# The tenth weight chunk of a feed-forward's down product as seven block products

## The chip, the cores and the metric

One core of one Trainium2 chip. The metric is the device time of one execution in microseconds (us), as the median of several runs; lower is better. The core's engines work side by side, each through its own list of instructions in program order: TensorE (PE: matmuls and the weight loads PEld), VectorE (DVE), ScalarE (ACT), GpSimd (POOL), and SyncE (SP), which issues most DMA transfers.

## The reference, cut to what matters

A decoder layer on 256 tokens of width 1024: pooling and attention heads, cross-attention, then a gated feed-forward of inner width 2816, each followed by a residual and a layer norm. The change touches the last product only:

```python
def swiglu(h, w_gate, w_up, w_down):
    return (jax.nn.silu(h @ w_gate) * (h @ w_up)) @ w_down

h = layer_norm(DEEPNORM_ALPHA * h + swiglu(h, w_gate[l], w_up[l], w_down[l]), ln3_g[l], ln3_b[l])
```

All tensors are float32. The kernel keeps that accuracy by splitting each operand into a high part (a cast to a shorter format, by ScalarE) and a low part (the operand minus its high part, by VectorE); one product then is three matmuls: high by high, high by low, low by high.

## The kernel before

**Tiles of the last product.** The inner width 2816 is cut into 11 chunks c = 0 to 10 of 256, each two row groups of 128 of `w_down`. The output is four pieces, C11 and C12 (tokens 0 to 127, left and right 512 columns), C21 and C22 (tokens 128 to 255). For a chunk the gated activations are four 128x128 blocks A11, A12, A21, A22 (token half, row group), the weights four 128x512 blocks B11, B12, B21, B22 (row group, column half). Done plainly, a chunk is eight block products, two for each piece.

**Seven products.** Chunks 0 to 8 (`SEVEN = 9`) use a scheme with seven. Three go to shared sums and are `shared_products(c)` together with A11·B11: four products from two prepared tiles x and y (left half of x is B11, its right half a sum of blocks; y holds two sums). `four(c, c+1)` makes the two products of the plain lower row (A12·B21 into C11, a token sum S4 by B22 into C12), `fourth` the one of A22 with a fourth weight sum into C21. The token sums S1 to S4 are formed by GpSimd (`token_sums`, lines 1098 to 1103) and split by ScalarE and VectorE (`token_sums_split`, `fourth_split`). The weight sums are formed in place by `Stream.sums` (lines 84 to 101): two casts of 512 columns and one of 1024 on ScalarE, six VectorE operations of 512 columns and one of 1024. `merge()` adds the shared sums up into `merged[0..3]` for the four pieces. Chunks 9 and 10 are plain: their four row groups run as `rest` through each piece at the end of `down()`, C22 in two column pieces of 256.

**Order of the weight work.** `Stream` holds one list of items in the order in which their tiles are prepared: `whole` (a row group: load, cast, low part), `sums` and `made` (the two tiles of a pair of rows), `home` (the tile of a fourth sum, kept meanwhile in a free buffer: those of chunks 0 to 7 in the norm's buffers `r`, `g`, `b`, that of chunk 8 in a raw buffer). Each product calls `ws.get`, and this calls `tick`, which prepares the next item only while fewer than `AHEAD = 9` tiles lie ahead of those used up; a `sums` needs room for two. Raw rows have 7 buffers, and `fetch` issues a load on SyncE's queue as soon as one counts as free. A tile wN is item N, and its parts are wNh (high), wNl (low), wNr (raw). Here w115 to w118 are the last weights of gate and up, w119 and w120 the sums of chunk 8, w121 onwards is down.

**Gate and up, then down.** A loop over c makes the gated chunk c on TensorE (48 matmuls of 512 columns), and behind it `shared_products(c - 2)`. Its last turn is c = 10. Then `down()` is stepped with `run(dn, 1)`, one product a step, and a table `events` puts splits, the return of the last gated chunk (`gated_in`) and parts of `merge` ahead of given steps. Behind the seven-product chunks, two VectorE additions (lines 1273 and 1274) put `merged` into the banks of C12 and C21 in place; then the rest is run piece by piece: C11, C12, the fourth products of chunks 4 to 7 (`LATE = 4`), C21, C22 in two halves. Each piece's layer norm follows on VectorE while TensorE runs the next.

**Buffers that matter.** `sg` (gated), `sraw` (raw token sums), `S` (split sums) and `u` (merged) share one ring of 6 buffers of tag `pr`, in the order in which they are made.

Of the kernel before, what the change touches and what calls it, by code (L numbers as in the profile page):

```python
# [17 lines left out]
T = S // P  # L18
# [6 lines left out]
NFC = DFF // CW  # L25
# [9 lines left out]
BUSY = 7  # L35
SEVEN, LAG, LATE = 9, 2, 4
GROUPED = 3
# [6 lines left out]
class Stream:  # L44


    def __init__(self, nc, pool):
        self.nc, self.pool = nc, pool
        self.src, self.raws, self.tiles, self.homes = [], [], [], []
        self.loads, self.splits = {}, {}  # L50
        self.used, self.held = 0, True
        self.pace, self.asked = 1, 0
        self.cuts, self.steps = {}, {}
        self.items, self.freed, self.rest = [], 0, {}
        self.kept = set()

# [73 lines left out]
    def prepare(self, upto, now=False):  # L130
        nc = self.nc
        while len(self.tiles) < min(upto, len(self.items)):
# [6 lines left out]
            if kind == "whole":  # L139
                self.fetch(r + 1, nc.sync)  # L140
                raw = self.raws[r]
                hi = self.pool.tile(list(raw.shape), F32R, tag="hi", name=f"w{i}h")
                lo = self.pool.tile(list(raw.shape), F32R, tag="lo", name=f"w{i}l")
                whole = [slice(0, raw.shape[2])]
                casts, subs = self.steps.get(r, (whole, whole))
                for s in casts:
                    nc.scalar.copy(hi[:, :, s], raw[:, :, s])
                for s in subs:
                    nc.vector.tensor_sub(lo[:, :, s], raw[:, :, s], r32(hi[:, :, s]))
                self.tiles.append((hi, lo))  # L150
                self.freed = r + 1
            elif kind == "sums":
                self.fetch(r + 2, nc.sync)
                self.tiles += self.sums(i, r)
                self.freed = r + (1 if r in self.kept else 2)
            else:
                raw, (hi, lo) = r(), self.part(i)
                self.freed += len(self.kept)
                self.kept.clear()
# [50 lines left out]
def decoder_layer(  # L210
# [68 lines left out]

    c_gu, c_sums = [], []  # L280
    for c in range(NFC):
        c_gu.append(ws.add(w_gu[c], 4))
        n = c - LAG
        if 0 <= n < SEVEN:
            c_sums.append(ws.add_sums([row(2 * n), row(2 * n + 1)], (lambda n=n: t4_home(n)) if n < SEVEN - 1 else None))
    c_t4, c_low = {}, {}
    c_t4[SEVEN - 1] = ws.add_home(lambda: ws.rest[ws.items[c_sums[-1][0][0]][1]]())
    c_low[SEVEN - 1] = ws.add(row(2 * SEVEN - 1), 1)
    for n in range(0, SEVEN - 1, 2):
        home = lambda n=n: t4[n // 2]  # L290
        if n < LATE:
            c_t4[n] = ws.add_home(home)
        for c in (n, n + 1):
            c_low[c] = ws.add(row(2 * c + 1), 1)
        if n >= LATE:
            c_t4[n] = ws.add_home(home)
    c_dn = {c: [ws.add(row(2 * c + f), 1) for f in range(2)] for c in range(SEVEN, NFC)}


# [791 lines left out]
    def token_sums(c):  # L1091
# [9 lines left out]
        own = s_raw[c][:, :, 3, :]  # L1101
        s4_raw = own if c == SEVEN - 1 else s_raw["fourth"][:, c].rearrange("p (i b) -> p i b", i=4)
        nc.gpsimd.tensor_sub(s4_raw, a12, s2)  # L1103

    def token_sums_split(c):
        hl = [sp.tile([P, 4, P], F32R, name=f"S{n}", tag="pr", bufs=PR_BUFS) for n in range(2)]
        sums_of[c] = [(hl[0][:, m], hl[1][:, m]) for m in range(3)]
        n = 3
        if c == SEVEN - 1:
            s4[c], n = (hl[0][:, 3], hl[1][:, 3]), 4  # L1110
# [66 lines left out]
    for c in range(1, NFC):  # L1177
# [6 lines left out]
        if c > 1:  # L1184
            gated_split(c - 2)
            if c - 2 < SEVEN:
                token_sums(c - 2)
        run(gu, 2)
        gated_in(c - 1)
        run(gu, 1)  # L1190
        if 0 <= c - 2 < SEVEN:
            token_sums_split(c - 2)
# [7 lines left out]
        if c == NFC - 1:  # L1200
            gated_out(c)
            residual(1)
        if 0 <= c - LAG < SEVEN:
            shared_products(c - LAG)
# [30 lines left out]
    def merge():  # L1235

        p1, p5, p6, p7 = shared
        for t in range(T):
            norms.append(Norm(3, h2[:, t, :]))

# [16 lines left out]
    def down():  # L1257

        yield from fourth(SEVEN - 1, SEVEN)
        yield from four(SEVEN - 1, SEVEN)  # L1260
        for c in range(0, SEVEN - 1, 2):
            if c < LATE:
                yield from fourth(c, c + 2)
            yield from four(c, c + 2)
        load_norm("g", 3, ln3_g)()
        load_norm("b", 3, ln3_b)()
# [8 lines left out]
        for piece in (*PIECES[:3], (1, 512, LAST), (1, LAST, D)):  # L1275
            t, c0, c1 = piece
            if piece == PIECES[2]:
                for c in range(LATE, SEVEN - 1, 2):
                    yield from fourth(c, c + 2)
# [136 lines left out]
```

## Time and profile before

| | us |
|---|---|
| median of 3 runs | 364.32 (364.13 to 364.88) |
| the profiled execution | 364.02 |
| its span, first to last instruction | 362.2 |
| TensorE busy | 356.8 (98%) |
| VectorE busy | 313.1 (86%) |
| ScalarE busy | 201.9 (56%) |
| GpSimd busy | 61.0 (17%) |

All times in the rows are of the one profiled execution, counted from the start of its span. Matmuls are pipelined, so that a row of 0.39 us is the time of one from issue to its modelled end; the distance from one start to the next is what it takes of TensorE's time. A mean busy share is taken over stages with different limits; the timelines of the engines show single instructions, and in brackets how long the engine stood idle before one and what ended that.

### The profile page before, as it was taken

Reading aid. Unit: us, or ns where it says so; the run is one execution under the profiler, and the core shown is the slowest. Engines: PE = TensorE matmul, PEld = TensorE weight load, DVE = VectorE, ACT = ScalarE, POOL = GpSimd, SP = SyncE. Lnnn points to the kernel's source line nnn. Section 1 sums busy time; section 2 is a strip of 40 time slices with the busy share of each in tenths; the row PEclk is TensorE's granted clock in tenths of the full one; section 3 lists DMA queues with packets and bytes.
Section 4 is the critical chain, followed back from the end, with each engine's and each line's share of the span. In section 5 each row is a group of like instructions: output and inputs, shape, how many; then the busy total and the mean of one; then the engine's idle time right before and its main releaser. Section 6 shows DMA issues by size and latency. Waiting matters only on the chain.

```text
span 362.2 us, 5435 instructions
## 1 busy us (share of the span) xinstructions
PE 356.8 (98%) x1843; PEld 304.4 (84%) x1843; DVE 313.1 (86%) x477; ACT 201.9 (56%) x317; POOL 61.0 (17%) x82
## 2 busy tenths in 40 slices
PE   8999999999999999999999999999999999999995
PEld 7887888888888899988888888888888888888884
DVE  5878999985999888775879989999998999879984
ACT  5857776375362765465037636744754754679301
POOL 1000009400000003320110024225303413400000
PEclk9999999999999999999999999999999999999999
DMA  7997388799936996943107887888879779658211
GB/s 247 419 419 281 116 286 314 227 329 316 371 148 208 375 373 219 340 137 135 58 0 239 320 283 243 292 293 302 297 253 346 246 256 313 218 172 260 85 58 58
DMA packets 35771, 89.22 MB, mean 246 GB/s; under 512 B 4256, under 2 KB 14368, under 8 KB 35616
## 3 DMA queue, kind: packets, MB, share of 16 engines
q1 hardware_dynamic: 34544, 86.92, 68.5%
q0 software_dynamic: 624, 1.57, 1.3%
q10 hardware_dynamic: 576, 0.39, 0.3%
q8 instruction: 14, 0.23, 0.2%
q14 instruction: 13, 0.11, 0.1%
HBM read 81.53 MB, written 7.34 MB: 245 GB/s over the span
## 4 chain that ended last, share of the span: by engine, by line
PE 98%; DMA 1%; ACT 0%; ACTq 0%; issue 0%
PE pg L376 11%; PE pg L375 11%; PE pg L374 11%; PE pxq L392 6%; PE pqk L548 6%; PE acc L374 6%; PE acc L376 6%; PE acc L375 6%; PE pxk L418 4%; PE x L376 2%; PE x L375 2%; PE x L374 2%; PE pxk L414 2%; PE pu L418 2%; PE xv L376 2%; PE xv L375 2%
## 5 line engine op out<-in xcount | busy, mean ns | idle before, releaser
L1098 POOL TENSOR_TENSOR sraw<-gr 128x128 f32<-128x128 f32 x9 | 8.7, 962 | 94.8 <-DMA gr<-gd 69.7
L847 POOL TENSOR_TENSOR rs<-mv,mhalf 128x1 f32<-128x1 f32 x6 | 4.4, 731 | 104.3 <-DVE mv L845 104.3
L703 POOL TENSOR_TENSOR win<-upad 128x271 f32<-128x271 f32 x4 | 3.5, 882 | 52.5 <-DVE upad L737 52.5
L478 ACT CAST h2Th<-tp 128x512 fp32r<-128x512 f32 x4 | 2.4, 588 | 14.5 <-PE tp L489 14.5
L1099 POOL TENSOR_TENSOR sraw<-sraw,gr 128x128 f32<-128x128 f32 x9 | 10.2, 1134 | 0.7
L1078 ACT ACTIVATE sg<-pg 128x256 f32<-128x256 f32 x22 | 7.8, 379 | 2.8 <-PE pg L376 2.7
L479 DVE TENSOR_TENSOR gTl<-gr,gTh 128x512 fp32r<-128x512 f32 x11 | 8.6, 780 | 0.7 <-ACT gTh L478 0.7
L478 ACT CAST gTh<-gr 128x512 fp32r<-128x512 f32 x11 | 6.8, 614 | 3.7 <-DMA gr<-gd 3.7
L1100 POOL TENSOR_TENSOR sraw<-gr 128x128 f32<-128x128 f32 x9 | 8.5, 945 | 0.0
L1079 DVE TENSOR_TENSOR sg<-sg,pg 128x256 f32<-128x256 f32 x22 | 8.3, 413 | 0.1
L510 POOL DMA_DIRECT2D xr<-xd x12 | 6.6, 554 | 8.7 <-DMA xd<-xs 6.3
L607 ACT ACTIVATE pr<-pr,mx 128x256 f32<-128x256 f32 (+1 forms) x12 | 5.5, 460 | 4.5 <-DVE mx L653 4.5
L607 ACT ACTIVATE xpr<-xs,mx 128x256 f32<-128x256 f32 x8 | 3.7, 470 | 7.6 <-DVE mx L618 7.6
L499 DVE STREAM_TRANSPOSE gs<-sg 128x512 f32<-128x512 f32 x11 | 7.7, 701 | 0.1
L478 ACT CAST S<-sraw 128x384 fp32r<-128x384 f32 (+1 forms) x9 | 4.7, 523 | 5.0 <-POOL sraw L1100 5.0
L502 POOL DMA_DIRECT2D xd<-xs x3 | 1.9, 629 | 33.4 <-DVE xs L499 33.4
L1336 ACT ACTIVATE minus<-ident 128x128 f32<-128x128 f32 x1 | 0.3, 311 | 12.8 <-DVE r L858 12.8
L852 DVE SCALAR_TENSOR_TENSOR r<-r,mv,g 128x512 f32<-128x512 f32 (+1 forms) x10 | 7.0, 727 | 0.2
L838 DVE BATCH_NORM_STATS2 st<-r 128x6 f32<-128x512 f32 (+1 forms) x10 | 6.4, 637 | 0.3
L1103 POOL TENSOR_TENSOR S<-gr,sraw 128x128 f32<-128x128 f32 x8 | 6.6, 828 | 0.0
L748 ACT COPY pr<-pxk 128x256 f32<-128x256 f32 x8 | 2.6, 376 | 7.2 <-PE pxk L414 7.2
L981 PE MATMUL xs<-xkTh,xq 128*128 128x256 f32 x32 | 6.4, 283 | 0.0
(1363 smaller groups left out, 1409.2 us busy)
## 6 DMA issues: line engine op xcount, KB each, us to landing
gd<-gs SPq DMA_DIRECT2D x11, 256.0 KB, 5.6
gr<-gd SPq DMA_DIRECT2D x44, 64.0 KB, 2.0
pd<-ps SPq DMA_DIRECT2D x4, 384.0 KB, 4.1
pt<-pd SPq DMA_DIRECT2D x16, 96.0 KB, 5.7
g<-in_ln_g SPq DMA_DIRECT2D x3, 512.0 KB, 5.4
b<-in_ln_b SPq DMA_DIRECT2D x3, 512.0 KB, 7.2
wr<-in_w_qkv SPq DMA_DIRECT2D x5, 256.0 KB, 4.6
mr<-in_mem_t SPq DMA_DIRECT2D x1, 1024.0 KB, 11.8
```

The lines of the kernel that those rows point to most:

```text
L374: nc.tensor.matmul(ps, wa, ya, start=start, stop=False, skip_group_check=part)
L375: nc.tensor.matmul(ps, wa, yb, start=False, stop=False, skip_group_check=part)
L376: nc.tensor.matmul(ps, wb, ya, start=False, stop=stop, skip_group_check=part)
L392: nc.tensor.matmul(pss[f], w[:, s], y, start=k == 0 and f == 0 and n == 0, stop=k == KD - 1 and n == 2, skip_group_check=True)
L418: nc.tensor.matmul(pss[f], hi[:, s], both, start=k == 0, stop=False, skip_group_check=True)
L478: nc.scalar.copy(h, ps)
L479: nc.vector.tensor_sub(l, ps, r32(h))
L548: nc.tensor.matmul(qk[i][f][:, n], w[:, c * P:(c + 1) * P], both[:, n], start=k == 0 and n.start == 0 and (n.stop == 2 or part in first), ...
L607: nc.scalar.activation(dst[:, j, :], src[:, j, :], AF.Exp, bias=mx[:, j:j + 1], scale=sign, accum_out=sm[:, j:j + 1])
L1098: nc.gpsimd.tensor_add(s1, a21, a22)
L1099: nc.gpsimd.tensor_sub(s2, s1, a11)
L1100: nc.gpsimd.tensor_sub(s3, a11, a21)
```

## The change

Chunk 9 goes through seven products as well (`SEVEN = 10`), with chunk 10 alone left plain. Its weight sums stand in the middle of down's list, behind the lower rows of chunks 0 to 3, and its fourth sum stays in a raw buffer, as that of chunk 8 does. Its token sums are issued right behind the last gated chunk, its four shared products behind those of chunk 3. The homes of chunks 0 to 3 move from the start of down to its end, and all fourth products of chunks 0 to 7 now run together ahead of C21. The `events` get new steps, and the norm objects are made later. A choice of GpSimd for low parts is added, whose set stays empty.

```diff
-SEVEN, LAG, LATE = 9, 2, 4
+SEVEN, LAG, PAIRED, ASIDE = 10, 2, 8, 9
...
-                    nc.vector.tensor_sub(lo[:, :, s], raw[:, :, s], r32(hi[:, :, s]))
+                    (nc.gpsimd if i in self.helped else nc.vector).tensor_sub(lo[:, :, s], raw[:, :, s], r32(hi[:, :, s]))
...
     c_gu, c_sums = [], []
+
+    def add_sums(n):
+        c_sums.append(ws.add_sums([row(2 * n), row(2 * n + 1)], (lambda: t4_home(n)) if n < PAIRED else None))
+
     for c in range(NFC):
         c_gu.append(ws.add(w_gu[c], 4))
-        n = c - LAG
-        if 0 <= n < SEVEN:
-            c_sums.append(ws.add_sums([row(2 * n), row(2 * n + 1)], (lambda n=n: t4_home(n)) if n < SEVEN - 1 else None))
+        if c >= LAG:
+            add_sums(c - LAG)
     c_t4, c_low = {}, {}
...
-    for n in range(0, SEVEN - 1, 2):
-        home = lambda n=n: t4[n // 2]
-        if n < LATE:
-            c_t4[n] = ws.add_home(home)
-        for c in (n, n + 1):
-            c_low[c] = ws.add(row(2 * c + 1), 1)
-        if n >= LATE:
-            c_t4[n] = ws.add_home(home)
...
+    add_fourth(PAIRED)
+    add_low(PAIRED)
+    for n in range(PAIRED):
+        add_low(n)
+        if n == 3:
+            add_sums(ASIDE)
+            add_fourth(ASIDE)
+            add_low(ASIDE)
+    add_fourth(4)
+    add_fourth(6)
     c_dn = {c: [ws.add(row(2 * c + f), 1) for f in range(2)] for c in range(SEVEN, NFC)}
+    add_fourth(0)
+    add_fourth(2)
...
         if c == NFC - 1:
             gated_out(c)
             residual(1)
-        if 0 <= c - LAG < SEVEN:
+            token_sums(ASIDE)
+        if c >= LAG:
             shared_products(c - LAG)
...
-        yield from fourth(SEVEN - 1, SEVEN)
-        yield from four(SEVEN - 1, SEVEN)
-        for c in range(0, SEVEN - 1, 2):
-            if c < LATE:
-                yield from fourth(c, c + 2)
+        yield from fourth(PAIRED, PAIRED + 1)
+        yield from four(PAIRED, PAIRED + 1)
+        for c in range(0, PAIRED, 2):
             yield from four(c, c + 2)
+            if c == 2:
+                shared_products(ASIDE)
+                yield from fourth(ASIDE, ASIDE + 1)
+                yield from four(ASIDE, ASIDE + 1)
...
             if piece == PIECES[2]:
-                for c in range(LATE, SEVEN - 1, 2):
+                for c in (4, 6, 0, 2):
                     yield from fourth(c, c + 2)
...
     events = {
-        4: lambda: fourth_split(4, SEVEN - 1), 5: lambda: gated_in(NFC - 1), 6: lambda: gated_split(NFC - 2),
-        12: lambda: gated_split(NFC - 1),
+        3: lambda: gated_split(ASIDE), 5: lambda: gated_in(NFC - 1), 7: lambda: token_sums_split(ASIDE),
+        11: lambda: fourth_split(4, PAIRED), 13: lambda: gated_split(NFC - 1),
     }
-    events.update({step: lambda: run(parts, 1) for step in (8, 16, 17)})
-    for step in range(23):
+    events.update({step: lambda: run(parts, 1) for step in (15, 18, 19)})
+    for step in range(22):
...
     until(dn)
+    norms += [Norm(3, h2[:, t, :]) for t in range(T)]
```

## Rows read from the trace of the kernel before

**Rows 1.** The page's engine line and the shares of its chain that ended last.

```profile
PE 356.8 (98%) x1843; PEld 304.4 (84%) x1843; DVE 313.1 (86%) x477; ACT 201.9 (56%) x317; POOL 61.0 (17%) x82
PE 98%; DMA 1%; ACT 0%; ACTq 0%; issue 0%
```

**Rows 2.** One stretch of down: busy us by engine, granted clock, DMA share, GB/s.

```profile
335.00:340.00 5.00, 5.00 (x23) 4.13 (x22) 5.00 (x6) 3.47 (x4) 0.00 (x0) 1.00 0.45 159
```

**Rows 3.** VectorE's timeline in down: start us, us, line, tiles, wait before it.

```profile
324.31 0.71 DVE L499 STREAM_TRANSPOSE gs<-sg 128x512 f32<-128x512 f32 x1
325.36 1.23 DVE L149 TENSOR_TENSOR w127l<-w124r,w127h 128x1024 fp32r<-128x1024 f32 x1 [0.33 <-ACT w127h L147]
342.59 1.28 DVE L1274 TENSOR_TENSOR acc<-u,acc 128x512 f32<-128x512 f32 x2
344.52 0.42 DVE L1303 TENSOR_TENSOR r<-u,acc 128x256 f32<-128x256 f32 x1 [0.65 <-PE acc L1286]
```

**Rows 4.** TensorE's timeline: down, C11, C12, C22, the first matmul behind them, the last.

```profile
325.96 0.39 PE L374 MATMUL acc<-w121h,gTh 128*128 128x512 f32 x1
341.60 0.39 PE L1284 MATMUL acc<-w135h,gTh 128*128 128x512 f32 x1
344.32 0.39 PE L1284 MATMUL acc<-w135h,gTh 128*128 128x512 f32 x1
352.48 0.28 PE L1284 MATMUL acc<-w135h,gTh 128*128 128x256 f32 x1
355.35 1.02 PE L1350 MATMUL left<-r,ident 128*128 128x256 f32 x4
357.80 0.59 PE L1358 MATMUL out<-r,diag 128*128 128x256 f32 x2
```

**Rows 5.** VectorE's timeline: first operation of chunk 8's sums, first operation behind them.

```profile
305.10 0.69 DVE L92 TENSOR_TENSOR w119l<-w119r,w119h 128x512 fp32r<-128x512 f32 x1
310.35 0.74 DVE L1079 TENSOR_TENSOR sg<-sg,pg 128x256 f32<-128x256 f32 x2
```

**Rows 6.** VectorE's timeline: splits of 512 and of 1024 columns with GpSimd idle.

```profile
332.78 0.68 DVE L479 TENSOR_TENSOR gTl<-gr,gTh 128x512 fp32r<-128x512 f32 x1
333.38 1.22 DVE L149 TENSOR_TENSOR w133l<-w129r,w133h 128x1024 fp32r<-128x1024 f32 x1
```

**Rows 7.** ScalarE's timeline: a cast of 512 columns.

```profile
329.16 0.61 ACT L478 CAST S<-S 128x512 fp32r<-128x512 f32 x1
```

**Rows 8.** VectorE's timeline: splits of 1024 and of 512 columns in gate and up.

```profile
247.18 1.48 DVE L149 TENSOR_TENSOR w93l<-w93r,w93h 128x1024 fp32r<-128x1024 f32 x1
250.41 0.95 DVE L479 TENSOR_TENSOR gTl<-gr,gTh 128x512 fp32r<-128x512 f32 x1
```

**Rows 9.** GpSimd's timeline: one operation of the token sums beside them.

```profile
247.66 1.33 POOL L1099 TENSOR_TENSOR sraw<-sraw,gr 128x128 f32<-128x128 f32 x1
```

**Rows 10.** VectorE's timeline in the tail.

```profile
350.13 1.52 DVE L858 SCALAR_TENSOR_TENSOR r<-r,rs,b 128x512 f32<-128x512 f32 x3
352.68 0.43 DVE L838 BATCH_NORM_STATS2 st<-acc 128x6 f32<-128x256 f32 x1 [1.02 <-PE acc L1286]
354.15 0.42 DVE L838 BATCH_NORM_STATS2 st<-acc 128x6 f32<-128x256 f32 x1
355.55 0.43 DVE L838 BATCH_NORM_STATS2 st<-acc 128x6 f32<-128x256 f32 x1 [0.98 <-PE acc L1286]
```

**Rows 11.** SyncE's queue: the transfers back of the last gated chunk.

```profile
329.31 1.79 SPq L510 DMA_DIRECT2D gr<-gd  x4
```

**Rows 12.** DMA issues, 305 to 350: times, KB each, us from issue to landing.

```profile
gr<-gd SPq DMA_DIRECT2D x12, 64.0 KB, 3.0
b<-in_ln_b SPq DMA_DIRECT2D x1, 512.0 KB, 3.6
```

**Rows 13.** Granted clock behind the last matmul (columns as in rows 2).

```profile
361.00:361.50 0.50, 0.00 (x0) 0.00 (x0) 0.00 (x0) 0.00 (x0) 0.00 (x0) 1.00 0.00 0
361.50:362.20 0.70, 0.00 (x0) 0.00 (x0) 0.00 (x0) 0.00 (x0) 0.00 (x0) 0.88 0.00 0
```

More of the change, by code (lines that the diff above doesn't have):

```diff
@@ L54, in __init__ @@
         self.items, self.freed, self.rest = [], 0, {}
-        self.kept = set()
+        self.kept, self.helped = set(), set()
     def add(self, src, parts=2):
@@ L157, in prepare @@
                 raw, (hi, lo) = r(), self.part(i)
-                self.freed += len(self.kept)
-                self.kept.clear()
+                gone = {r for r in self.kept if r < self.freed}
+                self.freed += len(gone)
+                self.kept -= gone
                 s = slice(0, raw.shape[2])
@@ L280, in decoder_layer, with add_fourth, add_low @@
     c_gu, c_sums = [], []
+    def add_sums(n):
+        c_sums.append(ws.add_sums([row(2 * n), row(2 * n + 1)], (lambda: t4_home(n)) if n < PAIRED else None))
     for c in range(NFC):
         c_gu.append(ws.add(w_gu[c], 4))
-        n = c - LAG
-        if 0 <= n < SEVEN:
-            c_sums.append(ws.add_sums([row(2 * n), row(2 * n + 1)], (lambda n=n: t4_home(n)) if n < SEVEN - 1 else None))
+        if c >= LAG:
+            add_sums(c - LAG)
     c_t4, c_low = {}, {}
-    c_t4[SEVEN - 1] = ws.add_home(lambda: ws.rest[ws.items[c_sums[-1][0][0]][1]]())
-    c_low[SEVEN - 1] = ws.add(row(2 * SEVEN - 1), 1)
-    for n in range(0, SEVEN - 1, 2):
-        home = lambda n=n: t4[n // 2]
-        if n < LATE:
-            c_t4[n] = ws.add_home(home)
-        for c in (n, n + 1):
-            c_low[c] = ws.add(row(2 * c + 1), 1)
-        if n >= LATE:
-            c_t4[n] = ws.add_home(home)
+    def add_fourth(n):
+        if n < PAIRED:
+            c_t4[n] = ws.add_home(lambda: t4[n // 2])
+        else:
+            c_t4[n] = ws.add_home(lambda: ws.rest[ws.items[c_sums[n][0][0]][1]]())
+    def add_low(n):
+        c_low[n] = ws.add(row(2 * n + 1), 1)
+    add_fourth(PAIRED)
[8 more added lines that the diff above has]
+    add_fourth(6)
     c_dn = {c: [ws.add(row(2 * c + f), 1) for f in range(2)] for c in range(SEVEN, NFC)}
+    add_fourth(0)
+    add_fourth(2)
     xt = ap.tile([P, T, D], F32, tag="a8", name="xt")
@@ L1101, in token_sums @@
         own = s_raw[c][:, :, 3, :]
-        s4_raw = own if c == SEVEN - 1 else s_raw["fourth"][:, c].rearrange("p (i b) -> p i b", i=4)
+        s4_raw = own if c >= PAIRED else s_raw["fourth"][:, c].rearrange("p (i b) -> p i b", i=4)
         nc.gpsimd.tensor_sub(s4_raw, a12, s2)
@@ L1108, in token_sums_split @@
         n = 3
-        if c == SEVEN - 1:
+        if c >= PAIRED:
             s4[c], n = (hl[0][:, 3], hl[1][:, 3]), 4
@@ L1185, in decoder_layer @@
             gated_split(c - 2)
-            if c - 2 < SEVEN:
-                token_sums(c - 2)
+            token_sums(c - 2)
         run(gu, 2)
@@ L1190, in decoder_layer @@
         run(gu, 1)
-        if 0 <= c - 2 < SEVEN:
+        if c > 1:
             token_sums_split(c - 2)
@@ L1237, in merge @@
         p1, p5, p6, p7 = shared
-        for t in range(T):
-            norms.append(Norm(3, h2[:, t, :]))
         def u(i):
```

## The prediction, written before the changed kernel had run

> **What bounds the kernel now.** I read the page's first and fourth parts first: TensorE is busy 98% of the span and 98% of the chain that ended last is its matmuls [rows 1]. So a matmul taken out is worth its full time only if no other engine is close behind. The stretches of down show who is: between 335 and 340 us VectorE is busy 5.00 of 5.00 us, ScalarE 3.47, and GpSimd not at all [rows 2]. VectorE's list for down [rows 3] then tells how close. It ends the transpose of the last gated chunk at 324.31 + 0.71 = 325.02, waits 0.33 us for a cast, and from 325.36 works with no gap up to the two in-place additions of line 1274, which end at 342.59 + 1.28 = 343.87. Only behind them does it wait for TensorE, 0.65 us. The first addition (C12) ends near 343.23; TensorE's first matmul into C12 behind it starts at 344.32 [rows 4]. So the slack of VectorE in down is 344.32 - 343.23 = 1.1 us, whatever its average share. That number decides this case.
>
> **TensorE's own sum.** Twelve matmuls of 512 columns run from 341.60 to 344.32, which is 0.2267 us each; 24 of 256 columns from 352.48 to 355.35, 0.1196 us each [rows 4]. The plain chunk 9 had 2 row groups in each piece: 3 pieces x 2 x 3 = 18 matmuls of 512 and 2 x 2 x 3 = 12 of 256, so 4.08 + 1.44 = 5.52 us. As seven products it has 21 of 512, 4.76 us. Gain: 0.76 us. By that alone the C22 pieces would end at 354.59 instead of 355.35. This is an upper bound: 0.21% of the time, and about 0.2% is what a measurement of this kernel can tell from no change.
>
> **VectorE's sum.** The sums of one pair of weight rows (seven instructions) took from 305.10 to 310.35, 5.25 us [rows 5]. The low part of a 1024-column tile takes 1.14 us from its start to the next start (twelve follow each other in down), one of 512 columns 0.60 us (332.78 to 333.38) [rows 6]; a merge addition of 512 columns is counted like it, at 0.60. Chunk 9 adds the sums (5.25), the low part of its fourth block (0.60), of its plain lower row (1.14) and of its token sums (0.60), and drops two plain rows (2.28): net +5.31 us. The check of these steps on the kernel before: 12 tiles x 1.14 + 3 splits x 0.60 + 3 merges x 0.60 + 0.64 = 17.92, from 325.36 to 343.28; the trace has 343.23.
>
> None of this can be made early. A tile is prepared only while fewer than nine are ahead of use, and the sums need two free places, so they are issued at the first product with w120, the last but one ahead of down, where the kernel before issued the tile w128. Before that point low parts of rows stand where homes stood, tile for tile, at equal cost. ScalarE's waits that leave VectorE idle ahead of 325 stay as they are.
>
> So from 325.02 (the first operation needs only a half cast, 0.61 us [rows 7], so the wait of 0.33 us goes): sums to 330.27; fourth block of chunk 9, 330.87; its lower row, 332.01; gated split of chunk 9, 332.61; rows of chunks 4 and 5, 334.89; token-sum split of chunk 9, 335.49; rows 6 and 7, 337.77; the other fourth sums, 338.37; homes of 4 and 6 and the two plain rows, 342.93; gated split of chunk 10, 343.53; home 0, first merge, home 2, two merges, 347.61; first addition of line 1274, 348.25. That is 11 x 1.14 + 5 x 0.60 + 3 x 0.60 + 5.25 + 0.64 = 23.23 us.
>
> **The unknown price: GpSimd beside the sums.** In the kernel before, no weight sums ever ran while GpSimd formed token sums. Now they do: the buffer of token sums 9 is the one that the transpose reads until 325.02, so GpSimd's four operations start just there. The nearest rows: with GpSimd running, a low part of 1024 columns took 1.48 us and a split of 512 took 0.95 [rows 8], against 1.22 and 0.68 alone [rows 6]; so an overlap costs 0.27 us, and a GpSimd operation was drawn out to 1.33 us [rows 9]. Over the chunks of gate and up, two or three of the four operations met such a VectorE instruction, the rest fell on a transpose or a wait. Bounds: 0.27 us (one) to 1.07 (four); no overlap at all is excluded because VectorE hardly pauses there, a gain because an overlap only ever lengthens rows. I take 0.80 (three), since the sums leave few pauses. The Trainium skill ("GPSIMD Engine Reference", 1. Specifications) says that GpSimd shares its SBUF interfaces with VectorE, in contention with instructions that have two SBUF inputs; all seven operations of the sums have two. By that rule all four GpSimd operations would be met, an estimate of 1.07 and 0.27 us on top of the forecast; the trace shows two or three of four.
>
> With 0.80, the first addition of line 1274 ends at 349.05, the second at 349.69.
>
> **What TensorE then meets.** Counted in products of 3 x 0.2267 = 0.68 us from 325.96 [rows 4], product 12 (token sum S2 of chunk 9) is due at 334.12 and its third matmul, which reads the low part, at 334.57. That low part is there at 335.49 + 0.80 + about 0.08 = 336.4: a first stall of 1.8 us. Products 13 to 25 and C11 follow; C12 is ready to start at 345.00 + 1.8 = 346.8. But line 1274 rewrites C12's bank in place, so C12 waits until 349.1: a second stall of 2.3 us. Queued behind it on TensorE is all that is left: C12 (6 matmuls), the fourth products of chunks 4, 6, 0 and 2 (24), C21 (6), together 36 x 0.2267 = 8.16, and C22 in two halves, 12 x 0.1196 = 1.44. It ends at 358.70, against 355.35: +3.35 us.
>
> **The tail.** VectorE's work from its first C11 operation to the last scaling of the first token half took 344.52 to 350.13 + 1.52 = 351.65 [rows 3, 10], 7.13 us; now 349.69 to 356.82. C21 is done at 357.26, and VectorE's statistics start 0.20 behind (352.48 and 352.68 before): 357.46. They and a product take 1.47 (352.68 to 354.15), then one statistic of C22's first half, some 0.40; only then the last statistic, at 359.33, where TensorE would have allowed 358.9. Before, this one started at 355.55 after a wait of 0.98 us [rows 10]. Halving the C22 pieces thus costs 0.4 us, since VectorE is late there. What follows (line 1354 on, the stores) is unchanged. End: +3.78 us.
>
> **Edits that cost nothing.** SyncE: the raw rows of chunk 10 now wait until the sums and the fourth block of chunk 9 have read their buffers (to about 331.7), and the four transfers of the last gated chunk, issued at 329.31 before [rows 11], queue behind them until about 332; with a landing of 3.0 us [rows 12] they are there by 336, and VectorE comes to their split at 343.7. Without that cover the split would stall C11. The two norm vectors go out behind homes 4 and 6, at about 340.4 and 341.5; with a landing of 3.6 us for the second [rows 12], and even with twice that, they are there by 349, used from 353. The extra 0.5 MB of rows falls into a stretch where the DMA engines are busy 0.45 of the time [rows 2]. ScalarE: one cast more of each size, on an engine with 1.5 of 5 us free [rows 2]. The later birth of the norm objects only moves an allocation. The GpSimd choice in the stream is never taken: its set stays empty.
>
> **Sum.** The profiled execution took 364.02 us with a span of 362.2; the median of the runs is 364.32, 0.30 more. 364.02 + 3.78 = 367.80 for such an execution, and 368.1 as a median.
>
> **Rivals.**
> 1. VectorE waits more than I count: its waits for casts were up to 0.9 us ahead of down, contention may reach 1.07, and the stalled TensorE frees tile places later, which ScalarE's casts wait for (I have them about 1 us ahead of VectorE). 369.0 to 371. Chance 0.13.
> 2. The addition of line 1274 does not hold TensorE (or is off the path). Against it: it writes the bank that C12 adds to. Even so the queue of VectorE sets the end: 356.82 + 1.47 + 0.40 = 358.69 for the last statistic, +3.1, 367.4. Chance 0.05, inside the range.
> 3. The other side: VectorE is not the bound, since its added work goes where it idles. It has 0.33 + 1.1 us before C12, so this holds only if the added work is below about 1.8 us (with the 0.68 us by which C12 moves later); the rows price it at 5.3 to 6.4. If so, 0.76 us gained and 0.4 lost in the tail give 363.96 (no change), or 363.56 if the tail takes it too, -0.21%. Chance 0.06, a third of it faster.
> 4. The clock. In the kernel before, TensorE's last matmul starts at 357.80 and takes 0.59 [rows 4]; the granted clock was still 1.00 up to 361.50, 3 us behind it, and 0.88 after that [rows 13]; stalls of 1.8 and 2.3 us are shorter. Were it to fall to the lower level of 1.2 GHz behind the second stall for all that is left, 9.6 us of matmuls would double: 377.7. Chance 0.02. The Trainium skill ("TensorE: Matmul & The Clock Gate", HAM oscillation) has idle gaps of TensorE make it restart slow; by that rule a stall is paid twice, and only a run can show whether these are long enough.
> The forecast has the rest, 0.74, at 367.3 to 368.9.
>
> **Range and chances.** 367.0 to 369.3: contention from none to four overlaps gives 367.3 to 368.4, one more wait of 0.9 us the upper end. Below lies mostly rival 3 and a VectorE somewhat quicker than counted, above half of rival 1 and the clock. Faster by over 0.2%: 0.02, within: 0.04, slower: 0.94.
>
> **What would show it.** Right: VectorE without a gap from 325 to about 349.7; the sums w127/w128 start at 325.0 and take 5.3 to 6.4 us; TensorE idle near 334.6 for about 1.8 us on a low part of S, and near 347 for about 2.3 us on line 1274; the last statistic 3.8 us later than before; TensorE's matmul time in down 0.76 us less. Wrong: a VectorE that idles between 325 and 345, TensorE without stalls, sums issued earlier, or a granted clock below 1.00 before the stores.

## The result

The changed kernel took 368.40 us as the median of five executions (368.20 to 371.30) against 364.32 before. The medians differ by a factor of 1.0112; taken over all executions the ratio is 1.0129, with a 95% interval of 1.0107 to 1.0152. The forecast of 368.1 us, its range and its sign held.

The execution that the profiler recorded is the longest of the five, 371.30 us with a span of 369.5, so its rows have to be read with care. First the page's line of engines and the shares of its chain; [rows 1] are the same lines of before.

```profile
PE 360.0 (97%) x1834; PEld 305.8 (83%) x1834; DVE 318.9 (86%) x485; ACT 204.2 (55%) x321; POOL 61.6 (17%) x86
PE 73%; DVE 11%; DMA 8%; issue 3%; ACT 3%; SPq 1%; DVEq 0%; ACTq 0%
```

TensorE has its nine matmuls fewer (1834 for 1843), VectorE has eight instructions more. VectorE's share of busy time says nothing of the change: it is 86% before and after. The chain says more, but only a part of it is the change. TensorE's matmuls were 98% of it and are now 73%, and VectorE has come into it with 11%. In this execution a matmul at 87 us waits for a transfer, and there the chain leaves TensorE and runs back through transfers and other engines almost to the start of the span (start us, us, what):

```profile
57.72 6.21 DMA w29r<-in_w_out
83.71 3.23 DMA pt<-pd
```

Of VectorE's share some 23 us lie ahead of 100 us, where the code is that of before, and 17 us from 325 us on. Two other profiles of the experiments below, without that detour, show what down does to the chain: TensorE 88% and 91%, VectorE 6% and 5% (without token sums, and with the early split).

The longest waits of TensorE (line, tile, what it waited for, us in total, times, longest). Before there was one wait of 0.8 us in the first 6 us, for a cast, and one of its own queue; in the lines quoted here the code has moved, and line 1274 is now 1290, 1284 and 1286 are 1300 and 1302, 374 to 376 are 390 to 392, 838 is 854.

```profile
PE acc L1300 <- DVE acc L1290: 1.9, 1, 1.9
PE x L392 <- DVE S L495: 1.6, 1, 1.6
PE po L706 <- DMA pt<-pd: 0.5, 1, 0.5
PE pqk L564 <- DVE w6l L149: 0.4, 1, 0.4
```

The two upper lines are the two forecast stalls. The two lower ones lie ahead of down. VectorE's list through the sums (start us, us, line, tiles), which in [rows 3] began with the transpose at 324.31:

```profile
326.16 0.71 DVE L515 STREAM_TRANSPOSE gs<-sg 128x512 f32<-128x512 f32 x1
326.80 0.67 DVE L92 TENSOR_TENSOR w127l<-w126r,w127h 128x512 fp32r<-128x512 f32 x1
327.50 0.69 DVE L93 TENSOR_TENSOR w126r<-w126r 128x512 f32<-128x512 f32 x1
328.23 0.69 DVE L94 TENSOR_TENSOR w126r<-w127r,w126r 128x512 f32<-128x512 f32 x1
328.96 0.83 DVE L96 TENSOR_TENSOR w127r<-w127r,w126r 128x512 f32<-128x512 f32 x1
329.82 0.84 DVE L97 TENSOR_TENSOR w127r<-w127r 128x512 f32<-128x512 f32 x1
330.58 1.48 DVE L99 TENSOR_TENSOR w128l<-w126r,w128h 128x1024 fp32r<-128x1024 f32 x1
331.99 0.95 DVE L100 TENSOR_TENSOR w127l<-w127r,w127h 128x512 fp32r<-128x512 f32 x1
332.86 0.68 DVE L163 TENSOR_TENSOR w129l<-w127r,w129h 128x512 fp32r<-128x512 f32 x1
...
350.16 1.28 DVE L1290 TENSOR_TENSOR acc<-u,acc 128x512 f32<-128x512 f32 x2
```

And what TensorE meets (wait before the row in brackets):

```profile
336.20 0.39 PE L391 MATMUL x<-w127l,S 128*128 128x512 f32 x1
338.21 0.50 PE L392 MATMUL x<-w127h,S 128*128 128x512 f32 x1 [1.62 <-DVE S L495]
...
348.56 0.39 PE L1302 MATMUL acc<-w138h,gTl 128*128 128x512 f32 x1
350.89 0.57 PE L1300 MATMUL acc<-w137h,gTh 128*128 128x512 f32 x1 [1.95 <-DVE acc L1290]
351.26 0.63 PE L1301 MATMUL acc<-w137l,gTh 128*128 128x512 f32 x1
351.69 0.63 PE L1302 MATMUL acc<-w137h,gTl 128*128 128x512 f32 x1
...
360.79 0.28 PE L1300 MATMUL acc<-w137h,gTh 128*128 128x256 f32 x1
```

The sums run from 326.80 to 332.86, 6.06 us. The first addition of line 1290 ends near 350.16 + 0.64 = 350.80, which lets C12 go at 350.89. The first stall is 338.21 - (336.20 + 0.23) = 1.8 us, the second 350.89 - (348.56 + 0.23) = 2.1 us.

Two things make this execution longer than the three that took 368.2 to 368.4. The transpose starts 326.16 - 324.31 = 1.85 us later than in [rows 3]: that is lost ahead of everything the change touches. The two small waits above are part of it. Of the 1.85 us, 1.05 are lost in the first 30 us, where the first weight tiles come later (the row on w6l starts at 14.35 us, against 13.41 before), and some 0.7 at the matmuls of `po` that wait for the transfer `pt<-pd` (87.17 us, against 85.37). The other thing is seen behind the second stall: matmuls of 512 columns now start 0.43 us apart (351.26, 351.69), not 0.2267. The stretches there (window, busy us of TensorE, its loads, VectorE, ScalarE, GpSimd, granted clock, DMA share, GB/s):

```profile
350.00:351.00 1.00, 0.10 (x1) 0.11 (x1) 1.00 (x3) 0.00 (x0) 0.00 (x0) 1.00 0.00 0
351.00:352.00 1.00, 1.00 (x3) 0.83 (x4) 0.96 (x3) 0.00 (x0) 0.00 (x0) 0.60 0.00 0
352.00:353.00 1.00, 1.00 (x4) 0.71 (x4) 0.93 (x4) 0.00 (x0) 0.00 (x0) 0.50 0.00 0
353.00:354.00 1.00, 1.00 (x4) 0.81 (x3) 0.96 (x3) 0.00 (x0) 0.00 (x0) 0.50 0.00 0
354.00:355.00 1.00, 1.00 (x5) 0.78 (x4) 1.00 (x4) 0.00 (x0) 0.00 (x0) 0.70 0.00 0
355.00:356.00 1.00, 1.00 (x6) 0.82 (x5) 0.93 (x3) 0.00 (x0) 0.36 (x1) 1.00 0.00 0
```

For some 3 us the granted clock is 0.50, the lower level of 1.2 GHz; then it is back. From C12 to the start of C22, 36 matmuls, TensorE takes 360.79 - 350.89 = 9.90 us; in the run without token sums below, where the clock stayed up, the same 36 take 357.01 - 348.71 = 8.30 us. So the clock cost 1.60 us here. The forecast for a profiled execution, 367.80, with the 1.85 us lost ahead of down and these 1.60, makes 371.25; it took 371.30.

The mean granted clock was 0.994 in the two executions above 369 us (371.30 and 369.59) and 0.999 to 1.000 in the other three. So it falls in some executions only. The second of the two has no profile; it is 1.2 us above the other three.

### The profile page after: what moved, and what is told of

The parts are those of the page before. It is cut to its first block, busy times and chain, and to the rows that moved or that the text cites. A ratio compares the mean times of both kernels' runs of the same rounds, so it can differ in the third digit from the quotient of the medians.

```text
span 369.5 us, 5444 instructions
## 1 busy us (share of the span) xinstructions
PE 360.0 (97%) x1834; PEld 305.8 (83%) x1834; DVE 318.9 (86%) x485; ACT 204.2 (55%) x321; POOL 61.6 (17%) x86
## 3 DMA queue, kind: packets, MB, share of 16 engines
q0 software_dynamic: 624, 1.57, 1.3%
## 4 chain that ended last, share of the span: by engine, by line
PE 73%; DVE 11%; DMA 8%; issue 3%; ACT 3%; SPq 1%; DVEq 0%; ACTq 0%
PE pg L392 11%; PE pg L391 11%; PE pg L390 11%; PE pxq L408 6%; PE acc L390 4%; PE acc L391 4%; PE acc L392 4%; PE pqk L564 4%; DMA w35r<-in_w_xkv 2%; DMA pt<-pd 2%; PE x L391 2%; PE xv L391 2%; PE xv L390 2%; PE x L392 2%; PE x L390 2%
## 5 line engine op out<-in xcount | busy, mean ns | idle before, releaser
L1114 POOL TENSOR_TENSOR sraw<-gr 128x128 f32<-128x128 f32 x10 | 8.4, 835 | 108.8 <-DMA gr<-gd 90.0
L1115 POOL TENSOR_TENSOR sraw<-sraw,gr 128x128 f32<-128x128 f32 x10 | 11.8, 1180 | 0.8
L1116 POOL TENSOR_TENSOR sraw<-gr 128x128 f32<-128x128 f32 x10 | 7.0, 700 | 0.0
L495 DVE TENSOR_TENSOR S<-sraw,S 128x384 fp32r<-128x384 f32 (+1 forms) x10 | 5.8, 576 | 1.3 <-ACT S L494 1.3
```

Of the source, the lines that this page charges most:

```text
L495: nc.vector.tensor_sub(l, ps, r32(h))
L1114: nc.gpsimd.tensor_add(s1, a21, a22)
L1115: nc.gpsimd.tensor_sub(s2, s1, a11)
```

## The experiments

Each ran against the kernel before on its own chip, where that took 364.37 to 364.52 us as a median. Theory A, the one of the prediction: VectorE's queue through down sets the time, by two dependencies of TensorE (the low part of token sum S2, and the in-place addition into C12). Its rivals are put to the test one by one.

**GpSimd's share.** GpSimd's four operations for chunk 9 are left out, and the token sums of chunk 8 stand in, so GpSimd is idle beside the weight sums:

```diff
-            token_sums(ASIDE)
+            s_raw[ASIDE] = s_raw[ASIDE - 1]
```

> The changed kernel without GpSimd's four token sums of chunk 9; chunk 8's raw token sums are split in their place, so chunk 9's S products hold the wrong numbers. It measures what GpSimd beside the weight sums costs. Theory (GpSimd lengthens the sums by 0.8 us, and VectorE's queue passes all of it on): the sums take 5.25 us again, the first additions of line 1290 end 0.8 us earlier, and the time is 0.8 us below the changed kernel's 368.3: 367.5. Rival A (contention is there, but hidden behind something else): 368.3. Rival B (four overlaps of 0.27): 367.2.

It took 367.50 and 367.87 us with a mean granted clock of 0.998, and 368.96 twice with 0.993 and 0.995. The median, 368.41, is that of the changed kernel, so the medians do not show the gain; the two at 0.998 lie 0.3 to 0.9 us below the changed kernel's three at a full clock. The stalls show it. The profile is of the execution of 367.50; VectorE first,

```profile
325.45 0.67 DVE L92 TENSOR_TENSOR w127l<-w126r,w127h 128x512 fp32r<-128x512 f32 x1
...
330.68 0.69 DVE L163 TENSOR_TENSOR w129l<-w127r,w129h 128x512 fp32r<-128x512 f32 x1
...
347.97 1.28 DVE L1290 TENSOR_TENSOR acc<-u,acc 128x512 f32<-128x512 f32 x2
```

and TensorE's rows that begin behind a wait, with the first of C22:

```profile
336.03 0.50 PE L392 MATMUL x<-w127h,S 128*128 128x512 f32 x1 [0.79 <-DVE S L495]
348.71 0.50 PE L1300 MATMUL acc<-w137h,gTh 128*128 128x512 f32 x1 [1.96 <-DVE acc L1290]
...
357.01 0.28 PE L1300 MATMUL acc<-w137h,gTh 128*128 128x256 f32 x1
...
358.90 1.10 PE L1367 MATMUL left<-r,ident 128*128 128x256 f32 x4 [0.30 <-DVE r L1359]
```

The same seven instructions take 5.23 us, against 6.06: the GpSimd beside them costs 0.83 us. All of it comes off the first stall (0.79 us, from 1.62), since the second stays as it was (1.96, from 1.95). This is also the cleanest look at the forecast's sum: without the 0.80, and 0.51 us later because this execution comes to the transpose at 324.82 and not 324.31, the sum ends the first addition at 348.25 + 0.51 = 348.76. It ended near 347.97 + 0.64 = 348.61. For the whole execution the sum gives 367.80 - 0.80 + 0.51 = 367.51; it took 367.50.

The price is not fixed, as two runs further down show. With six low parts left out, GpSimd starts 0.4 us behind the transpose and meets four of the operations that only rewrite raw rows; these take 0.83 us for 0.69, and the sums 5.81 us, 0.58 more than with GpSimd idle. With the sums begun early it meets four low parts of 512 columns, 0.95 us for 0.68 and 0.87 for 0.60 to the next start, 1.08 in all. A row of each:

```profile
326.73 0.83 DVE L94 TENSOR_TENSOR w126r<-w127r,w126r 128x512 f32<-128x512 f32 x1
326.40 0.95 DVE L101 TENSOR_TENSOR w127l<-w127r,w127h 128x512 fp32r<-128x512 f32 x1
```

**The first stall.** The split of the token sums of chunk 9 goes from step 7 to step 3, beside the gated split:

```diff
-        3: lambda: gated_split(ASIDE), 5: lambda: gated_in(NFC - 1), 7: lambda: token_sums_split(ASIDE),
+        3: lambda: (gated_split(ASIDE), token_sums_split(ASIDE)), 5: lambda: gated_in(NFC - 1),
```

> The changed kernel with one event moved: the split of chunk 9's token sums stands beside its gated split at step 3, ahead of the low parts of chunks 4 and 5, not at step 7. It takes away TensorE's first stall (1.6 us in the trace of the changed kernel) and leaves VectorE's amount of work as it is. Theory (VectorE's queue sets the end, not TensorE's stalls): no stall at the shared products of chunk 9, the second stall grows from 2.0 to about 3.7 us, and the time stays at 368.3, within 0.3. Rival (each stall is paid for): 1.6 us less, 366.7.

It took 370.30 us (370.07 to 370.91), two more than expected. The first stall is gone and the second has taken it over, as expected; but the clock fell, in all four executions (mean 0.990 to 0.995). TensorE's only long wait:

```profile
349.31 0.80 PE L1300 MATMUL acc<-w137h,gTh 128*128 128x512 f32 x1 [3.46 <-DVE acc L1290]
```

and the stretches around it:

```profile
345.00:350.00 5.00, 1.54 (x6) 0.95 (x5) 5.00 (x8) 0.00 (x0) 0.00 (x0) 0.79 0.02 7
350.00:355.00 5.00, 5.00 (x14) 3.89 (x13) 4.79 (x13) 0.00 (x0) 0.55 (x1) 0.53 0.00 0
```

From 350 to 355 TensorE gets 14 rows done at 0.53. Whether the clock is the whole of the two us is put to the test next:

**The clock alone.** The same kernel with 28 matmuls of 256 columns that nothing uses, in the place of the stall (28 x 0.1196 = 3.35 us):

```diff
+            if piece == PIECES[1]:
+                hi = ws.at(rest[0], 0)[0]
+                for _ in range(FILL):
+                    nc.tensor.matmul(acc[1, LAST, D], gT[0][0][:, 0, :P], hi[:, :256], start=True, stop=True,
+                                     skip_group_check=True)
```

> The kernel with the early split (first stall gone, second 3.5 us), with 28 matmuls of 256 columns that no result uses put ahead of C12, about 3.4 us of work for TensorE in the second stall. In that kernel the granted clock was 0.79 and 0.53 in the two stretches of 5 us behind 345. Theory (what it lost against the changed kernel, 370.3 against 368.3, is the clock that falls while TensorE stands still): the granted clock stays at 1.00 and the time is 368.3, within 0.3. Rival (the loss lies in VectorE's or SyncE's order): 370.3.

It took 368.59 us (368.37 to 368.74), with a mean granted clock of 1.000 in all four. The same stretches:

```profile
345.00:350.00 5.00, 4.87 (x34) 4.44 (x35) 5.00 (x7) 0.00 (x0) 0.00 (x0) 1.00 0.05 19
350.00:355.00 5.00, 5.00 (x24) 4.08 (x23) 4.79 (x14) 0.00 (x0) 0.55 (x1) 1.00 0.00 0
```

VectorE's busy time is what it was (5.00 and 4.79), TensorE has 24 rows from 350 to 355 in place of 14. TensorE is given work for nothing and the kernel is 1.7 us faster: what the stall cost beyond its length was the clock. It also shows that removing the first stall is worth nothing: from the start of the transpose to the first in-place addition VectorE takes 24.00 us in the changed kernel, 24.05 with the early split and 23.99 with the stall filled, so C12 is let go no earlier.

**The order of the work without the seven products.** The kernel before, with chunk 9 left plain, but with the homes of chunks 0 and 2 at the end and all fourth products ahead of C21:

```diff
-    for n in range(0, SEVEN - 1, 2):
-        home = lambda n=n: t4[n // 2]
-        if n < LATE:
-            c_t4[n] = ws.add_home(home)
...
+    for c in range(SEVEN - 1):
+        c_low[c] = ws.add(row(2 * c + 1), 1)
+    add_fourth(4)
+    add_fourth(6)
     c_dn = {c: [ws.add(row(2 * c + f), 1) for f in range(2)] for c in range(SEVEN, NFC)}
+    add_fourth(0)
+    add_fourth(2)
...
-                for c in range(LATE, SEVEN - 1, 2):
+                for c in (4, 6, 0, 2):
```

> The kernel before with the changed order alone: chunk 9 stays plain, homes 0 and 2 are prepared last, and the fourth products of chunks 4, 6, 0 and 2 run together ahead of C21. VectorE's work is unchanged, but four products less of TensorE stand ahead of C12 (2.72 us), against VectorE's slack of 1.1 us there. Theory (C12 waits for the in-place addition): a stall of about 1.6 us ahead of C12 that stays to the end, 366.0. Rival (the order costs nothing, all of the change's loss is added VectorE work): 364.3.

It took 366.15 us (365.88 to 366.44), 1.0046 times before (1.0030 to 1.0063). In its profile TensorE waits 1.57 us for VectorE's addition into C12:

```profile
343.88 0.50 PE L1280 MATMUL acc<-w133h,gTh 128*128 128x512 f32 x1 [1.57 <-DVE acc L1270]
```

This follows from the prediction's own rows: the fourth products of chunks 0 and 2 are twelve matmuls, 12 x 0.2267 = 2.72 us, that stood ahead of C12 and now stand behind it, while VectorE still has to split both homes ahead of its addition. The slack of 1.1 us becomes -1.6. The prediction had this inside its "C12 is ready to start at" and did not name it: 1.8 us of the loss are there without the seven products.

**The seven products without the new order.** The opposite half: chunk 9 as in the changed kernel, the homes of 0 and 2 and their fourth products back in their old places, both splits of chunk 9 at step 7.

```diff
     for n in range(PAIRED):
+        if n in (0, 2):
+            add_fourth(n)
         add_low(n)
...
-                for c in (4, 6, 0, 2):
+                for c in (4, 6):
...
-        3: lambda: gated_split(ASIDE), 5: lambda: gated_in(NFC - 1), 7: lambda: token_sums_split(ASIDE),
-        11: lambda: fourth_split(4, PAIRED), 13: lambda: gated_split(NFC - 1),
+        7: lambda: (gated_split(ASIDE), token_sums_split(ASIDE)), 9: lambda: gated_in(NFC - 1),
+        15: lambda: fourth_split(4, PAIRED), 17: lambda: gated_split(NFC - 1),
```

> Chunk 9 as seven products, but in the order of the kernel before: homes 0 and 2 and the fourth products of chunks 0 to 3 stay at the start of down (2.72 us of TensorE ahead of C12 again), the events move with them, and both splits of chunk 9 stand at step 7. VectorE does the same work as in the changed kernel. Theory (VectorE's queue sets the end): no first stall, one of about 1.7 us ahead of C12; TensorE is through with C21 near 355, but VectorE still has to finish the first half's norm (7.1 us behind line 1290's additions) and comes to C21 only near 357; its last statistic is 3.4 us later than in the kernel before, 367.8. Rival (TensorE's stalls set the end): 356.3 against 355.35 for TensorE's end, so 365.3 to 365.8.

It took 368.22 us as the median of 367.99, 368.05, 368.38 and, with the clock at 0.995, 370.24. C12 now waits only 1.4 us, and the first stall is gone, yet the time is that of the changed kernel. What ends last has moved:

```profile
PE left L1369 <- DVE r L1361: 2.0, 1, 2.0
PE acc L1302 <- DVE acc L1292: 1.4, 1, 1.4
```

TensorE waits 2.0 us in the tail for VectorE's last vectors. It resembles rival 2, in which VectorE's queue sets the end although the addition holds TensorE less (367.4 by its sum; 368.0 here, in a kernel of another order). So the two halves cost 1.8 and 3.8 us alone and 4.1 together: they do not add up, because both meet the same queue of VectorE.

**Less work on VectorE in the middle of down.** The low parts of six tiles, 130 to 134 and 137, are left out; the high part stands in, so these weights count twice.

```diff
-                for s in subs:
+                for s in subs if i not in (130, 131, 132, 133, 134, 137) else ():
...
-                self.tiles.append((hi, lo))
+                self.tiles.append((hi, lo if i not in (130, 131, 132, 133, 134, 137) else hi))
```

> The changed kernel without six low parts of weight tiles on VectorE (lower rows of chunks 9, 4, 5, 6, 7 and one plain row); their high parts are used in their place, so the weights there are wrong in their last digits. ScalarE's casts, all transfers and all matmuls stay. VectorE has 6 x 1.14 = 6.8 us less to do. Theory (VectorE alone is what holds TensorE): both stalls are gone, what is left is TensorE's gain of 0.76 us less some 0.4 in the tail: 363.6 to 364.0. Rival (a transfer, ScalarE's casts or the order of buffers holds it too): above 365.

It took 365.44 us (365.30 to 365.73), well above the 363.6 to 364.0 of theory A. Six operations of 1.14 us less should have cleared both stalls; C12 still waited 1.30 us. VectorE's rows that begin behind a long wait:

```profile
333.93 0.69 DVE L495 TENSOR_TENSOR S<-sraw,S 128x512 fp32r<-128x512 f32 x1 [1.69 <-ACT S L494]
336.35 0.69 DVE L495 TENSOR_TENSOR S<-S,S 128x512 fp32r<-128x512 f32 x1 [1.73 <-ACT S L494]
```

and the stretches:

```profile
330.00:335.00 5.00, 5.00 (x23) 4.05 (x22) 2.94 (x5) 5.00 (x8) 0.00 (x0) 1.00 0.70 249
335.00:340.00 5.00, 5.00 (x23) 4.13 (x22) 3.05 (x3) 5.00 (x6) 0.00 (x0) 1.00 0.14 35
```

Now VectorE idles for ScalarE's casts, and ScalarE (fourth busy column) is full from 330 to 340. The engine behind VectorE was ScalarE, with little more to give: of the 6.8 us taken out of VectorE, about 4.2 us came back as waits for casts (1.69 and 1.73, and two more of 0.26 and 0.48). So the theory of VectorE alone does not hold here, and its rival does: ScalarE's casts hold the kernel too. The same was therefore tried where ScalarE has time.

**Less work on VectorE late in down.** The early split as above, and no low parts of the six tiles 135 to 140, which stand last in the queue ahead of the addition (their weights count twice).

```diff
+LEFT_OUT = range(135, 141)
...
-                for s in subs:
+                for s in subs if i not in LEFT_OUT else ():
...
-                self.tiles.append((hi, lo))
+                self.tiles.append((hi, hi if i in LEFT_OUT else lo))
```

> The kernel with the early split, without the low parts of the last six tiles (w135 to w140: the homes of chunks 4, 6, 0 and 2 and the two plain rows); their high parts stand in, so these weights count twice. VectorE has 6 x 1.14 = 6.8 us less, this time at the end of its list, where ScalarE's casts are some 4 us ahead of it and not close behind. It mends the experiment with six low parts left out, where VectorE waited 4.2 us for ScalarE and C12 still 1.3 us for VectorE. Theory (with VectorE out of the way TensorE's 0.76 us are there, less 0.4 in the tail, where C22's pieces are half as long): no stall in down, 363.6 to 364.1. Rival (something else holds the changed order back): above 364.5.

It took 364.19 us, the median of ten executions (363.54 to 364.75), against 364.52 for the kernel before in thirteen on that chip: 0.9989 times (0.9980 to 0.9999). TensorE has no stall in down, and VectorE waits for TensorE again:

```profile
344.43 1.29 DVE L1292 TENSOR_TENSOR acc<-u,acc 128x512 f32<-128x512 f32 x2 [0.20 <-PE acc L394]
353.95 0.43 DVE L856 BATCH_NORM_STATS2 st<-acc 128x6 f32<-128x256 f32 x1 [1.01 <-PE acc L1304]
```

So with VectorE out of the way the changed order and the seven products are worth 0.33 us, where the prediction's -0.76 and +0.4 in the tail make -0.36. The interval only just excludes a ratio of 1, the gain is a thousandth of the time, and the kernel that has it leaves work out.

**The sums begun early.** Four of the seven operations only rewrite raw rows; they are put into the last turn of gate and up, with one more buffer of 512 columns (`warm` is cut from 40 to 32 columns to make room).

```diff
+        for out, x, y in ((spare, b12, b11), (b12, b22, b12), (b22, b22, spare), (b21, b21, b22)):
+            self.nc.vector.tensor_sub(out, x, y)
+            yield
...
+        if c == NFC - 1:
+            early_sums = ws.begin(c_sums[ASIDE], sp.tile([P, 1, 512], F32, name="spare", bufs=1))
+            run(early_sums, 1)
```

> The changed kernel with the four in-place subtractions of chunk 9's weight sums begun in the last turn of gate and up, where VectorE idles 0.4 to 0.9 us ahead of each low part (they need no tile place, only a spare buffer of 512 columns); casts and low parts of the sums stay where they were. VectorE's work is the same to within one instruction; only its place changes. Theory (what costs is VectorE's work behind 325 us): the sums there take 2.4 us and not 5.25, the work ahead ends 0.4 us later, no first stall, a second one of 1.6 us, 365.8 to 366.2. Rival A (ScalarE's casts, found busy 5.00 of 5.00 between 330 and 340 without the six low parts, are close behind): 366.5 to 367.5. Rival B (what costs is the amount, wherever it stands): 368.3.

It took 366.44 us once with a clock of 0.998, and 367.78, 368.25 and 367.84 otherwise (median 367.81, 1.0089 times before). That lies above the theory's 365.8 to 366.2. The first stall is gone, C12 still waits 1.9 us, and in the profiled execution, one with 0.995, the clock falls behind it. The next run has 14 matmuls of 256 columns in the place of that stall, as above:

> The kernel with the sums begun early, with 14 matmuls of 256 columns that no result uses put ahead of C12 (1.7 us of work in a stall of 1.9). Without them one run took 366.44 at a mean granted clock of 0.998 and three took 367.78 to 368.25 at 0.995. Theory (that spread is the clock behind the stall, and VectorE's place saves 1.9 to 2.4 us): 366.2 to 366.6 in all runs. Rival (the spread has another cause, such as where the transfers fall): a spread of over 1 us again.

It took 366.00, 366.07, 366.55 and 367.79 us (median 366.31, 1.0058 times before, 1.0036 to 1.0081), with clocks of 0.998 to 1.000. One lies in the expected range, two are 0.1 to 0.2 us below it, and the fourth is 1.2 to 1.8 us longer than the others, at a full clock. So the spread of over 1 us that the rival expected is there, and the clock does not explain all of it; the cause stays open. By the medians the loss against the kernel before is 1.8 us here, against 4.1 for the changed kernel: some 2 us can be had back with the seven products in place.

**Low parts on GpSimd.** The branch that the change adds and leaves empty, with two tiles in its set:

```diff
-        self.kept, self.helped = set(), set()
+        self.kept, self.helped = set(), {133, 134}
```

> The changed kernel with its unused choice taken for two tiles: the low parts of the lower rows of chunks 6 and 7 (w133, w134) are formed by GpSimd, which has nothing else to do then. VectorE has 2 x 1.14 = 2.3 us less. Theory (GpSimd keeps VectorE from the memory while it works: 0.27 us for each 128 columns in the token sums, so 2.2 us for each of these tiles): 2 us slower, 370. Rival (an overlap costs 0.27 us an instruction, whatever its length): 2.3 - 0.5 = 1.7 us faster, 366.5.

It took 371.57 us (370.55 to 374.05). GpSimd's two rows:

```profile
335.10 3.46 POOL L149 TENSOR_TENSOR w133l<-w131r,w133h 128x1024 fp32r<-128x1024 f32 x1 [3.91 <-ACT w133h L147]
338.52 2.82 POOL L149 TENSOR_TENSOR w134l<-w132r,w134h 128x1024 fp32r<-128x1024 f32 x1
```

and VectorE's beside them:

```profile
336.28 2.83 DVE L495 TENSOR_TENSOR S<-sraw,S 128x512 fp32r<-128x512 f32 x1
339.03 2.86 DVE L495 TENSOR_TENSOR S<-S,S 128x512 fp32r<-128x512 f32 x1
341.81 1.21 DVE L163 TENSOR_TENSOR w135l<-t,w135h 128x1024 fp32r<-128x1024 f32 x1
```

VectorE's splits of 512 columns take 0.68 us elsewhere and 2.83 and 2.86 here: each ends some 0.55 us behind GpSimd's operation. The offload takes 2.3 us of subtractions from VectorE and gives back 4.3 us in these two splits, 2.15 us for each tile, which is the theory's 2.2. The first stall grew to 3.77 us, the second shrank to 0.48. The time lies 1.6 us above the theory's 370; the mean granted clock was 0.989 to 0.995 in all four executions (0.78 from 340 to 345 us in the profiled one), which the theory had left out.

No version with the whole computation beat the kernel before.

## Why the prediction was right

The bound, and the place where it bites, were read from the slack of VectorE at the addition into C12 (1.1 us), and the runs agree: leaving VectorE's queue as it is and removing a stall does not help (the early split), and shortening the queue helps until ScalarE or TensorE is next. By its steps:

- **VectorE's sum.** From the end of the transpose (326.87) to the end of the first addition (350.80) are 23.9 us; the sum with the contention is 23.23 + 0.80 = 24.03.
- **GpSimd's price.** 0.83 us measured as a difference of kernels, 0.80 taken. The size was right, the composition not, and that it came out so close is partly luck. Three overlaps of 0.27 were counted; four VectorE instructions were lengthened, the two low parts by 0.27 (to the next start 1.41 for 1.14, 0.87 for 0.60) and the two that only rewrite raw rows by some 0.14 (0.86 for 0.73, 0.76 for 0.61; the shorter ones from the run without token sums). Which four are met depends on when GpSimd starts, and that was not at the end of the transpose, as forecast, but 1.9 us behind it; in other runs the price was 0.58 and 1.08. The rule of the Trainium skill ("GPSIMD Engine Reference", 1. Specifications), that GpSimd's SBUF interfaces are contended with VectorE's two-input instructions, would have had all four met, which is what the rows show. The estimate of 1.07 us made from it was too high for the changed kernel, as two of the four instructions were rewrites, which lose half as much; why they do is not shown.
- **The stalls.** 1.8 and 2.1 us, forecast 1.8 and 2.3, on the tiles and lines named. In the execution without token sums the first addition is off by 0.15 us.
- **The tail.** Forecast +0.4, since VectorE's work behind C21 takes longer than the halved C22 pieces. In the execution without token sums TensorE waits 0.30 us there (for `r`), and the late tiles left out give -0.33 us in all where -0.36 was the sum.
- **What was to cost nothing.** The transfers and the norm vectors did not appear in any wait. ScalarE was priced too kindly, with "1.5 of 5 us free": the one stretch that was read has it, but in the same trace of before ScalarE is busy 4.97 of 5.00 us from 325 to 330 and 4.69 from 330 to 335; in the changed kernel it is 4.83 from 330 to 335. It cost nothing there because VectorE was later still; it took back most of the gain as soon as VectorE was faster.
- **The order.** Not a step of its own in the prediction, though in its sum; alone it costs 1.8 us.
- **What can be made early.** The prediction has it that none of the added work can. Four of the seven operations of the sums could, with a buffer of 512 columns; with the second stall filled as well, that is worth some 2 us.
- **Rival 3's bound.** Its terms, 0.33, 1.1 and 0.68, make 2.1 us and not 1.8. Nothing hangs on it, as the added work took over 5 us.
- **The clock.** This is the step that was wrong. Rival 4 got a chance of 0.02 and the price of everything left (377.7), argued from a clock still at 1.00 for 3 us behind the last matmul. The clock did fall, behind the second stall as named, but for some 3 us only and at 1.6 us in the profiled execution; a second of the five has the same mean clock. The event was likelier and far cheaper than I had it, and it is not in the forecast's sum. That the median held is in part luck: with one more execution of this kind it would have been some 369.6 us, above the range of 367.0 to 369.3. The Trainium skill ("TensorE: Matmul & The Clock Gate", HAM oscillation) has TensorE restart slow behind idle gaps. This trace agrees: 2.1 us of stall, then 1.60 us for the slower matmuls.

What stays open: why the first weight tiles and the transfer `pt<-pd` came later in the profiled execution, which makes its 1.85 us. Most of the other kernels run here show the wait for VectorE's w6l too, at 0.2 to 0.5 us, and the quiet executions left no profile. Open is also why the clock falls in some executions and not in others of the same kernel.

## What to carry to other kernels

Find the engine that comes second, and its slack at the one dependency where the first engine meets it; a change is paid there, instruction by instruction, and neither engine's busy share shows it. A gain of 0.76 us on TensorE was bought with 5.3 us of VectorE that had 1.1 us to spare. And ask the same of the third engine before trusting a remedy: here it was ScalarE, which took 4.2 of the 6.8 us that VectorE was spared.

## What the runs showed of the hardware

- After stalls of some 2 us TensorE's granted clock fell in some executions and not in others. By the mean clock (0.993 to 0.995 where it fell) it was two of five in the changed kernel, two of four without token sums and three of four with the sums begun early; one of four (0.995) with chunk 9 in the old order, where the waits were 1.4 and 2.0 us. With a stall of 3.5 us, and with one of 3.8, it fell in all four, and with one of 1.6 us in none of four. In the profiled executions it went to 0.50, the level of 1.2 GHz. It was back at 1.00 some 3 to 5 us after TensorE went on, and the 36 matmuls behind the stall took 9.9 us in two of them and 10.8 in the one with the longest stall before C12, against 8.3 at a full clock. With matmuls that nothing uses in the gap the mean clock was 0.998 to 1.000 in all eight executions.
- A GpSimd subtraction of 1024 columns took 2.82 to 3.46 us, against 1.22 for VectorE alone, and a VectorE split beside it 2.83 us for 0.68. Four GpSimd operations of 128 columns cost VectorE 0.58 to 1.08 us together: 0.27 us for each low part of a tile that they met, 0.14 for each operation that only rewrites raw rows.
